# A one-core hybrid layer kernel: convolution taps loaded by a step of their own, the four short vectors loaded and turned with the biases

## The chip, the cores and the metric

The kernel runs on one core of a Trainium2 chip. The metric is device time in microseconds (us) of one execution. The engines are TensorE (PE; its weight loads are listed as PEld), VectorE (DVE), ScalarE (ACT), GpSimd (POOL) and SyncE (SP). A row with a q behind the engine's name (SPq, ACTq) is work of that engine's queue: here the issue of a DMA.

## The reference

One layer of a diffusion backbone: tokens x (1024 x 1024, float32) and 256 context tokens are RMS-normalised and modulated by vectors computed from `c` and `c_ctx`; the result is projected; half of the width goes through a convolution module, the other half through attention; both are gated and projected out.

```python
mod = jax.nn.silu(c) @ w_mod + b_mod                  # w_mod: 1024 x 3072
shift, scale, gate = jnp.split(mod, 3, axis=-1)
u = rms_norm(x, norm_w) * (1.0 + scale) + shift
p = u @ w_in
...
def conformer_conv(glu_in, conv_w, conv_b, ln_w, ln_b, w_pw, b_pw):
    a, g = jnp.split(glu_in, 2, axis=-1)
    u = a * jax.nn.sigmoid(g)
    y = conv(u, conv_w) + conv_b                      # depthwise, 31 taps, 512 channels
    y = jax.nn.silu(layer_norm(y, ln_w, ln_b))
    return y @ w_pw + b_pw
```

The change concerns `conv_w` (31 x 512, the taps) and the four vectors of 512 numbers, `conv_b`, `conv_ln_w`, `conv_ln_b` and `b_pw`. The kernel needs them per channel, one channel to a partition, so it loads them as rows and turns them by a matmul against the identity.

## The kernel before

The program has a start, a projection stage, attention, and an output stage. Every matrix product is made of three float32r products: an operand is split into a high part (name ending in h, made by ACT) and a low part (ending in l, the difference, made by DVE or POOL).

The start does three things at once. It computes the modulation in eight groups of columns (numbered by j, 0 to 7), it normalises and turns the eight tiles of tokens, and it computes the first GLU product (tiles a and g) from each group j as soon as its modulated tokens exist. It is a list of steps, `START`, whose letters mean:

- L j loads the columns of `w_mod` of group j (tiles wm; from group 3 on wm3s, wm4s, ...; four DMAs each, issued by SP); T j splits them; C j multiplies them with silu(c) (tile mrow, L264); D j copies the row (mrs, on DVE), turns it (mcol) and adds the biases (modc).
- X loads four token tiles, Q and R normalise one. P turns one group of one half of the tokens (xt), U modulates and splits it (u, uh, ul), M multiplies it (a, g).
- W loads the weights of the first GLU block, S splits them.
- V (`vectors`) loads the taps (cwrow) and the four vectors (vrow), turns both into the PSUM tile pcw, and copies them to cw and vcol.

Steps ahead of the bar in `START` are kept in the order written. From the bar on, a scheduler with a cost model of its own orders the instructions of each engine, so that a change of one step can move others; engines then run their instructions strictly in that order. Before the list, `setup` loads c, c_ctx, b_mod and norm_w (tiles crow and brow) and turns them.

Each DMA that SP or ACT issues is given one of eight completion semaphores in turn, by the build (named DMAHW0 to DMAHW7 in the orders below; the _49 behind them is the same for all). The issue waits until the DMA that had this semaphore before has landed. So at most eight such DMAs are under way, small or large, and a queue whose next DMA has to wait holds up all that stands behind it on that engine. These semaphores are called lanes below.

The first taps run on DVE when the first GLU block is done (`glu`, L453 and L456), and vcol is read there, in the layer norm (L511) and behind the pointwise product (L534). In the output stage, ln_stats turns y (yt, L480), ln_swish turns the normalised n (nt, L509) and makes s, sh and sl; `pointwise` (pw, L531) reads these; out_mm (o, L820) is the last product.

Of the kernel before, what the change touches and what calls it, by code (L numbers as in the profile page):

```python
# [9 lines left out]
F32 = mybir.dt.float32  # L10
# [8 lines left out]
P = 128  # L19
# [7 lines left out]
CW = 31  # L27
PAD = (CW - 1) // 2
EPS = 1e-6
Q0, K0, ZA0, A0, G0, ZC0 = 0, 512, 768, 1280, 1792, 2304  # L30
# [42 lines left out]
START = (  # L73
# [7 lines left out]
class Layer:  # L81
# [56 lines left out]
    def setup(self):  # L138

        nc, a, cst = self.nc, self.a, self.cst  # L140
        row = lambda ap, n: ap.rearrange("o (r f) -> (o r) f", f=P)[0:n]
        crow = self.w2([16, P], "crow")
        brow = self.w2([24, P], "brow")
        nc.sync.dma_start(out=crow[0:8], in_=row(a["c"], 8))
        nc.scalar.dma_start(out=crow[8:16], in_=a["c_ctx"].rearrange("(r f) -> r f", f=P))
        nc.scalar.dma_start(out=brow[0:16], in_=row(a["b_mod"], 16))
        nc.scalar.dma_start(out=brow[16:24], in_=row(a["norm_w"], 8))
        self.ident = ident = cst.tile([P, P], F32, name="ident")
        make_identity(nc, ident)
# [15 lines left out]
        pb = self.bank("t", "pb")  # L165
        nc.tensor.transpose(out=pb[:, 0:24], in_=brow, identity=ident[0:24, 0:24])
        self.bcol = bcol = cst.tile([P, 24], F32, name="bcol")
        nc.vector.tensor_copy(out=bcol[:, 0:8], in_=pb[:, 0:8])
        nc.vector.tensor_scalar(out=bcol[:, 8:16], in0=pb[:, 8:16], scalar1=1.0, scalar2=None, op0=ALU.add)
        nc.vector.tensor_copy(out=bcol[:, 16:24], in_=pb[:, 16:24])  # L170
        self.modc = cst.tile([P, NK, 4], F32, name="modc")

    def vectors(self):

        nc, a, cst = self.nc, self.a, self.cst
        row = lambda ap, n: ap.rearrange("o (r f) -> (o r) f", f=P)[0:n]
        vrow = self.w2([16, P], "vrow")
        cwrow = self.w2([CW, 512], "cwrow")
        for i, n in enumerate(("conv_b", "conv_ln_w", "conv_ln_b", "b_pw")):
            nc.sync.dma_start(out=vrow[4 * i:4 * i + 4], in_=row(a[n], 4))  # L180
        nc.sync.dma_start(out=cwrow, in_=a["conv_w"].rearrange("o w c -> (o w) c"))
        pw = self.bank("t", "pcw")
        for b in range(4):
            nc.tensor.transpose(out=pw[:, b * 32:b * 32 + CW], in_=cwrow[:, b * P:(b + 1) * P],
                                identity=self.ident[0:CW, 0:CW])
        nc.tensor.transpose(out=pw[:, 128:144], in_=vrow, identity=self.ident[0:16, 0:16])
        self.cw = cst.tile([P, 4, 32], F32, name="cw")
        nc.vector.tensor_copy(out=self.cw[:, :, 0:CW],
                              in_=pw[:, 0:128].rearrange("p (b w) -> p b w", w=32)[:, :, 0:CW])
        self.vcol = cst.tile([P, 16], F32, name="vcol")  # L190
        nc.vector.tensor_copy(out=self.vcol, in_=pw[:, 128:144])

# [752 lines left out]
    def start(self, w_in):  # L945
# [18 lines left out]
        def scale(i):  # L964
# [3 lines left out]
                 "Q": lambda i: r.update({i: self.norm_stats(self.xs[i])}), "R": scale,  # L968
                 "P": self.turn_x, "V": self.vectors, "U": self.make_u, "M": mm}
        first, rest = START.split("|")  # L970
# [99 lines left out]
```

## Time and profile before

| what | value |
|---|---|
| median of 3 runs | 688.29 us (686.16 to 690.2) |
| the profiled execution | 690.57 us |
| its span in the profile | 688.8 us (1.77 us lie around it) |
| mean granted TensorE clock | 0.989 |

The profiled execution is 2.28 us above the median. The span is what the views below divide up. An engine's share of busy time is an average over stages that have different limits; for a change in the start, the rows of the start decide. In a row of a timeline the bracket says how long the engine was idle before it and what ended the wait.

### The profile page before, as it was taken

The page shows a single profiled execution, that of the slowest core. Times are in us where ns is not written, and L with a number is a line of the kernel's source. Part 1 is how long each engine was busy: PE and PEld are TensorE (multiplying, and loading weights), DVE is VectorE, ACT ScalarE, POOL GpSimd, SP SyncE. Part 2 cuts the span into 40 slices and gives each one's busy share as a digit, 9 for nine tenths or more (in the row PEclk, how much of TensorE's full clock was granted, in tenths as well). Part 3 has the DMA queues.
Part 4 walks back from the last instruction along what each step waited for, and adds up shares of the span by engine and source line. Part 5 has one row for each costly group of instructions (what it writes and reads, how often), then busy time and mean ns, then how long its engine had stood idle before and what let it go on. Part 6 is the DMA issues. An engine that isn't in the chain of part 4 may idle for free.

```text
span 688.8 us, 11008 instructions
## 1 busy us (share of the span) xinstructions
PE 654.2 (95%) x4259; PEld 576.0 (84%) x4259; DVE 537.1 (78%) x844; ACT 352.2 (51%) x578; POOL 330.5 (48%) x289
## 2 busy tenths in 40 slices
PE   5979999999999999998999999999999989999997
PEld 1457899888888999997899998888888868888886
DVE  2678789839999999867999999999999953545422
ACT  3644424555343112235888888888888744332100
POOL 1233813967329132885657666655665754201200
PEclk9999999999999999999999999999999999999999
DMA  8973320311653232000010001011100021233711
GB/s 276 314 212 98 118 62 1 93 30 62 214 183 123 76 104 67 31 1 1 1 32 1 19 23 53 1 31 32 32 1 1 1 93 30 83 101 124 258 62 46
DMA packets 51251, 53.28 MB, mean 77 GB/s; under 512 B 4521, under 2 KB 41697, under 8 KB 51200
## 3 DMA queue, kind: packets, MB, share of 16 engines
q1 hardware_dynamic: 51136, 52.58, 24.3%
q8 instruction: 33, 0.54, 0.3%
q14 instruction: 18, 0.15, 0.1%
q10 hardware_dynamic: 64, 0.02, 0.0%
HBM read 44.20 MB, written 8.39 MB: 76 GB/s over the span
## 4 chain that ended last, share of the span: by engine, by line
PE 66%; DVE 24%; DMA 3%; issue 3%; ACT 2%; SPq 1%; POOL 0%; DVEq 0%; ACTq 0%
PE o L820 12%; PE pv L715 8%; PE s L636 7%; PE pt L682 7%; DVE y L456 6%; PE g L386 6%; PE a L386 6%; PE kv L412 4%; DVE yp L456 4%; PE pw L531 3%; PE zc L386 3%; PE q L412 3%; DVE p L700 3%; DVE nm L654 2%; DMA wm<-in_w_mod 2%
## 5 line engine op out<-in xcount | busy, mean ns | idle before, releaser
L706 POOL TENSOR_TENSOR p<-raw,p 128x512 fp32r<-128x512 f32 x96 | 127.0, 1337 | 81.7 <-DVE p L700 71.1
L636 PE MATMUL s<-kT,qT 128*128 128x512 f32 (+1 forms) x384 | 101.6, 375 | 3.8 <-ACT e L672 3.7
L715 PE MATMUL pv<-p,v 128*128 128x256 f32 x640 | 103.4, 293 | 0.7 <-DVE mm L747 0.7
L456 DVE SCALAR_TENSOR_TENSOR yp<-up,cw,yp 128x1024 f32<-128x1024 f32 x77 | 99.1, 1287 | 1.9
L682 PE MATMUL pt<-ident,e 128*128 128x128 f32 x640 | 94.4, 275 | 1.1 <-DVE p L706 0.9
L672 ACT ACTIVATE e<-s,nm 128x1280 f32<-128x1280 f32 x64 | 85.0, 1328 | 14.6 <-DVE nm L665 14.3
L715 PEld LDWEIGHTS pv<-p,v 128*128 128x128 f32 x640 | 86.2, 189 | 4.4 <-DVE mm L747 1.5
L654 DVE TENSOR_REDUCE nm<-s 128x1 f32<-128x1024 f32 x64 | 77.7, 1214 | 0.5
L682 PEld LDWEIGHTS pt<-ident,e 128*128 128x128 f32 x640 | 74.1, 142 | 2.7 <-PE pv L715 1.2
L636 PEld LDWEIGHTS s<-kT,qT 128*128 128x128 f32 x384 | 63.5, 191 | 10.6 <-ACT e L672 4.7
L691 ACT ACTIVATE raw<-pt 128x512 f32<-128x512 f32 x96 | 57.2, 598 | 10.2 <-PE pt L682 5.7
L700 DVE CAST p<-raw 128x512 fp32r<-128x512 f32 x96 | 47.3, 520 | 1.9 <-ACT raw L691 1.2
L698 ACT ACTIVATE p<-pt 128x512 fp32r<-128x512 f32 x64 | 38.5, 601 | 11.6 <-PE pt L682 10.2
L706 DVE TENSOR_TENSOR p<-pt,p 128x512 fp32r<-128x512 f32 x64 | 40.9, 676 | 1.4 <-ACT p L698 1.4
L456 DVE SCALAR_TENSOR_TENSOR y<-up,cw,y 128x1024 f32<-128x1024 f32 x25 | 40.9, 1635 | 0.8
L833 DVE TENSOR_TENSOR r<-o,gb 128x512 f32<-128x512 f32 (+1 forms) x17 | 10.8, 656 | 31.3 <-PE o L820 31.3
L659 DVE TENSOR_REDUCE nm<-s 128x1 f32<-128x256 f32 x64 | 26.9, 421 | 9.0 <-PE s L636 7.7
L441 POOL TENSOR_TENSOR yz<-yz,ct 128x512 f32<-128x512 f32 x24 | 33.6, 1433 | 0.0
L123 POOL TENSOR_TENSOR qr<-qr,mhalf 128x8 f32<-128x8 f32 (+1 forms) x13 | 21.2, 1631 | 8.7 <-DVE qr L122 8.4
L116 POOL TENSOR_TENSOR ul<-u,uh 128x512 fp32r<-128x512 f32 x8 | 11.2, 1405 | 27.4 <-DVE uh L114 26.0
L440 ACT ACTIVATE ct<-up,cw 128x512 f32<-128x512 f32 x24 | 15.7, 713 | 12.4 <-DVE up L424 9.9
L665 DVE TENSOR_TENSOR nm<-nm 128x1 f32<-128x1 f32 x64 | 20.3, 317 | 1.6
(580 smaller groups left out, 1758.1 us busy)
## 6 DMA issues: line engine op xcount, KB each, us to landing
x<-in_x SPq DMA_DIRECT2D x8, 512.0 KB, 7.0
wg<-in_w_mod SPq DMA_DIRECT2D x8, 512.0 KB, 4.1
xr<-in_x SPq DMA_DIRECT2D x8, 512.0 KB, 9.0
out<-r SPq DMA_DIRECT2D x15, 256.0 KB, 2.2
wm<-in_w_mod SPq DMA_DIRECT2D x12, 256.0 KB, 6.1
zc_d<-zc SPq DMA_DIRECT2D x4, 512.0 KB, 3.2
za_d<-za SPq DMA_DIRECT2D x4, 512.0 KB, 3.9
zar<-za_d SPq DMA_DIRECT2D x4, 512.0 KB, 3.9
```

The source lines that it names most:

```text
L386: nc.tensor.matmul(acc[h], lhsT=ww, rhs=uu[k][:, h * 512:(h + 1) * 512], start=first and i == 0, stop=last and i == 2)
L412: self.nc.tensor.matmul(acc[:, t * 256:(t + 1) * 256], lhsT=x, rhs=y, start=k == 0 and i == 0, stop=k == NK - 1 and i == 2)
L456: nc.vector.scalar_tensor_tensor(out=out, in0=up[:, w:w + S], scalar=cw[:, w:w + 1], in1=y if w else st["y2"], op0=ALU.mult, op1=ALU.add)
L636: mm = nc.tensor.matmul(self.s5[:, s0 + k0:s0 + k0 + n], lhsT=qt[:, h % 4, t * P:(t + 1) * P], rhs=kT[:, w, k0:k0 + n], start=w == 0, stop ...
L654: r = self.nc.vector.reduce_max(out=nm[:, 0:1], in_=self.s5[:, 1536 * t:1536 * t + 1024], axis=AX.X, negate=True)
L672: ex = nc.scalar.activation(e, self.s5[:, t * KEYS:(t + 1) * KEYS], AF.Exp, bias=st["nm", t][:, 2:3], accum_out=st["z"][:, t:t + 1])
L682: nc.tensor.transpose(out=tp[:, i * 256 + t * P:i * 256 + (t + 1) * P], in_=st["e", t][:, (2 * k + i) * P:(2 * k + i + 1) * P], identity=s ...
L691: self.nc.scalar.activation(raw, st["T", k], AF.Copy)
L700: nc.vector.tensor_copy(out=st["p", k][:, 0], in_=st["T", k])
L706: eng.tensor_sub(out=p[:, 1], in0=st["T", k], in1=p[:, 0].bitcast(F32))
L715: nc.tensor.matmul(st["pv"][:, 0:256], lhsT=self.v[:, kt, u[1] // 4].rearrange("p w d -> p (w d)"), rhs=st["p", k][:, j, i * 256:(i + 1) * ...
L820: self.nc.tensor.matmul(o, lhsT=p, rhs=q, start=half == k == i == 0, stop=half == 1 and k == 3 and i == 2)
```

## The change

The step V is parted. A new step Y (`tap_rows`) only issues the DMA of the taps; it stands behind L2, the load of the third group of modulation columns, in the part of `START` whose order is kept. V (`taps`) turns the taps and copies them. The four vectors are loaded by `setup`, from ACT's queue, into sixteen more rows of brow; they are turned by the matmul that turns the biases, which now has 40 rows where it had 24, and are copied to vcol there.

```diff
--- before.py
+++ after.py
@@ -71,7 +71,7 @@
 MODF = 3
 TLO = ['dp', 'pp', 'pp', 'dd', 'dd', 'dd', 'pd', 'dd']
 START = (
-    "L0 X0 L1 Q0 C0 W0 X1 Q1 L2 D0 Q2 R2 R0 L3 L4 Q3 R3 S0 | R1 C1 P00 P10 U00 W1 Q5 D1 M00 Q6 Q7 Q4 U10 R5 R4 R6 "
+    "L0 X0 L1 Q0 C0 W0 X1 Q1 L2 Y D0 Q2 R2 R0 L3 L4 Q3 R3 S0 | R1 C1 P00 P10 U00 W1 Q5 D1 M00 Q6 Q7 Q4 U10 R5 R4 R6 "
     "P20 R7 C2 M10 T3 P01 P11 V D2 U01 M01 P21 U11 C3 L5 M11 T4 D3 U20 C4 T5 U21 M21 M20 D4 L6 P30 U30 M30 C5 S1 "
     "P31 D5 T6 U31 L7 M31 P40 P50 U40 P41 M40 U41 C6 T7 D6 U50 M41 C7 P60 P51 D7 U51 U60 M50 P61 U61 M60 M51 P70 "
     "U70 P71 M61 U71 M70 M71"
@@ -140,11 +140,13 @@
         nc, a, cst = self.nc, self.a, self.cst
         row = lambda ap, n: ap.rearrange("o (r f) -> (o r) f", f=P)[0:n]
         crow = self.w2([16, P], "crow")
-        brow = self.w2([24, P], "brow")
+        brow = self.w2([40, P], "brow")
         nc.sync.dma_start(out=crow[0:8], in_=row(a["c"], 8))
         nc.scalar.dma_start(out=crow[8:16], in_=a["c_ctx"].rearrange("(r f) -> r f", f=P))
         nc.scalar.dma_start(out=brow[0:16], in_=row(a["b_mod"], 16))
         nc.scalar.dma_start(out=brow[16:24], in_=row(a["norm_w"], 8))
+        for i, n in enumerate(("conv_b", "conv_ln_w", "conv_ln_b", "b_pw")):
+            nc.scalar.dma_start(out=brow[24 + 4 * i:28 + 4 * i], in_=row(a[n], 4))
         self.ident = ident = cst.tile([P, P], F32, name="ident")
         make_identity(nc, ident)
         self.identr = cst.tile([P, P], F32R, name="identr")
@@ -163,32 +165,30 @@
         nc.vector.tensor_copy(out=cv[:, 0], in_=scv)
         nc.vector.tensor_sub(out=cv[:, 1], in0=scv, in1=cv[:, 0].bitcast(F32))
         pb = self.bank("t", "pb")
-        nc.tensor.transpose(out=pb[:, 0:24], in_=brow, identity=ident[0:24, 0:24])
+        nc.tensor.transpose(out=pb[:, 0:40], in_=brow, identity=ident[0:40, 0:40])
         self.bcol = bcol = cst.tile([P, 24], F32, name="bcol")
         nc.vector.tensor_copy(out=bcol[:, 0:8], in_=pb[:, 0:8])
         nc.vector.tensor_scalar(out=bcol[:, 8:16], in0=pb[:, 8:16], scalar1=1.0, scalar2=None, op0=ALU.add)
         nc.vector.tensor_copy(out=bcol[:, 16:24], in_=pb[:, 16:24])
+        self.vcol = cst.tile([P, 16], F32, name="vcol")
+        nc.vector.tensor_copy(out=self.vcol, in_=pb[:, 24:40])
         self.modc = cst.tile([P, NK, 4], F32, name="modc")
 
-    def vectors(self):
-
-        nc, a, cst = self.nc, self.a, self.cst
-        row = lambda ap, n: ap.rearrange("o (r f) -> (o r) f", f=P)[0:n]
-        vrow = self.w2([16, P], "vrow")
-        cwrow = self.w2([CW, 512], "cwrow")
-        for i, n in enumerate(("conv_b", "conv_ln_w", "conv_ln_b", "b_pw")):
-            nc.sync.dma_start(out=vrow[4 * i:4 * i + 4], in_=row(a[n], 4))
-        nc.sync.dma_start(out=cwrow, in_=a["conv_w"].rearrange("o w c -> (o w) c"))
+    def tap_rows(self):
+
+        self.cwrow = self.w2([CW, 512], "cwrow")
+        self.nc.sync.dma_start(out=self.cwrow, in_=self.a["conv_w"].rearrange("o w c -> (o w) c"))
+
+    def taps(self):
+
+        nc = self.nc
         pw = self.bank("t", "pcw")
         for b in range(4):
-            nc.tensor.transpose(out=pw[:, b * 32:b * 32 + CW], in_=cwrow[:, b * P:(b + 1) * P],
+            nc.tensor.transpose(out=pw[:, b * 32:b * 32 + CW], in_=self.cwrow[:, b * P:(b + 1) * P],
                                 identity=self.ident[0:CW, 0:CW])
-        nc.tensor.transpose(out=pw[:, 128:144], in_=vrow, identity=self.ident[0:16, 0:16])
-        self.cw = cst.tile([P, 4, 32], F32, name="cw")
+        self.cw = self.cst.tile([P, 4, 32], F32, name="cw")
         nc.vector.tensor_copy(out=self.cw[:, :, 0:CW],
                               in_=pw[:, 0:128].rearrange("p (b w) -> p b w", w=32)[:, :, 0:CW])
-        self.vcol = cst.tile([P, 16], F32, name="vcol")
-        nc.vector.tensor_copy(out=self.vcol, in_=pw[:, 128:144])
 
     def tables(self):
 
@@ -966,7 +966,7 @@
         steps = {"L": self.mod_load, "X": tokens, "W": lambda h: st.update({h: self.w_stage(w_in, wcol, "wglu0", h)}),
                  "S": split, "T": self.mod_split, "C": self.mod_mm, "D": self.mod_cols,
                  "Q": lambda i: r.update({i: self.norm_stats(self.xs[i])}), "R": scale,
-                 "P": self.turn_x, "V": self.vectors, "U": self.make_u, "M": mm}
+                 "P": self.turn_x, "Y": self.tap_rows, "V": self.taps, "U": self.make_u, "M": mm}
         first, rest = START.split("|")
         with self.tc.manual_schedule():
             for step in first.split():
```

What this does to the orders is shown at three places.

**The queues of DMAs.** First SP before, at the loads of wm4s (group 4), the vectors, the taps and the first loads of wm5s (group 5); a bracket names the semaphores that a row waits for, and four rows are left out in the middle:

```order
L215 DMA wm4s_202<-in_w_mod 128x4x128 [waits DMAHW6_49]
L215 DMA wm4s_202<-in_w_mod 128x4x128 [waits DMAHW7_49]
L215 DMA wm4s_205<-in_w_mod 128x4x128 [waits DMAHW0_49]
L215 DMA wm4s_205<-in_w_mod 128x4x128 [waits DMAHW1_49]
...
L180 DMA vrow<-in_conv_b 4x128 [waits DMAHW6_49,Activation_49]
L180 DMA vrow<-in_conv_ln_w 4x128 [waits DMAHW7_49]
L180 DMA vrow<-in_conv_ln_b 4x128 [waits DMAHW0_49]
L180 DMA vrow<-in_b_pw 4x128 [waits DMAHW1_49]
L181 DMA cwrow<-in_conv_w 31x512 [waits DMAHW2_49,DVE_49,PE_49]
L215 DMA wm5s_394<-in_w_mod 128x4x128 [waits DMAHW3_49]
L215 DMA wm5s_394<-in_w_mod 128x4x128 [waits DMAHW4_49]
```

And SP now, from the end of L2 on:

```order
L180 DMA cwrow<-in_conv_w 31x512 [waits DMAHW6_49]
L215 DMA wm3s_204<-in_w_mod 128x4x128 [waits DMAHW7_49]
...
L215 DMA wm4s_210<-in_w_mod 128x4x128 [waits DMAHW3_49]
L215 DMA wm4s_210<-in_w_mod 128x4x128 [waits DMAHW4_49]
L215 DMA wm4s_213<-in_w_mod 128x4x128 [waits DMAHW5_49]
L215 DMA wm4s_213<-in_w_mod 128x4x128 [waits DMAHW6_49]
...
L215 DMA wm5s_392<-in_w_mod 128x4x128 [waits DMAHW3_49]
L215 DMA wm5s_392<-in_w_mod 128x4x128 [waits DMAHW4_49]
L215 DMA wm5s_395<-in_w_mod 128x4x128 [waits DMAHW5_49]
L215 DMA wm5s_395<-in_w_mod 128x4x128 [waits DMAHW6_49]
```

The taps' row has moved up past the loads of groups 3 and 4; the four rows of vrow are gone from SP, and the four loads of wm5s stand on the lanes that the four loads of wm4s had. ACT's first rows before:

```order
L145 DMA crow<-in_c_ctx 8x128
L146 DMA brow<-in_b_mod 16x128
L147 DMA brow<-in_norm_w 8x128
L159 ACT_TABLE_LOAD
L159 ACTIVATE sc<-pc 128x16 [waits PE_49]
```

And now:

```order
L145 DMA crow<-in_c_ctx 8x128
L146 DMA brow<-in_b_mod 16x128
L147 DMA brow<-in_norm_w 8x128
L149 DMA brow<-in_conv_b 4x128
L149 DMA brow<-in_conv_ln_w 4x128 [waits DMAHW1_49]
L149 DMA brow<-in_conv_ln_b 4x128 [waits DMAHW3_49]
L149 DMA brow<-in_b_pw 4x128 [waits DMAHW5_49]
L161 ACT_TABLE_LOAD
L161 ACTIVATE sc<-pc 128x16 [waits PE_49]
```

Four DMAs have come in ahead of ACT's table load, and three of them wait for a lane: DMAHW1, 3 and 5 are those of c_ctx, b_mod and norm_w, in this order.

**PE at the turning of the taps**, before (a and g are the first GLU block, mcol turns the modulation of group 3, and the last two rows begin that of group 4):

```order
L386 MATMUL g_120<-ul_287,wglu00h 128x512
L386 MATMUL g_120<-uh_286,wglu00l 128x512
L386 MATMUL a_118<-ul_287,wglu00h 128x512
L386 MATMUL a_118<-uh_286,wglu00l 128x512
L184 MATMUL pcw<-ident,cwrow 128x31 x4
L186 MATMUL pcw<-ident,vrow 128x16
L276 MATMUL mcol_416<-ident,mrs_414 128x4 x2
L264 MATMUL mrow_429<-wm40h,chl 4x256
L264 MATMUL mrow_429<-wm40l,chl 4x256
```

And now, from the first GLU matmuls of group 0 on the second half of the tokens:

```order
L386 MATMUL g_126<-uh_248,wglu00h 128x512
L386 MATMUL a_124<-uh_248,wglu00h 128x512
L264 MATMUL mrow_375<-wm31h,chl 4x256
L187 MATMUL pcw<-ident,cwrow 128x31 x4
L386 MATMUL g_126<-ul_249,wglu00h 128x512
L386 MATMUL g_126<-uh_248,wglu00l 128x512
L386 MATMUL a_124<-ul_249,wglu00h 128x512
L386 MATMUL a_124<-uh_248,wglu00l 128x512
L264 MATMUL mrow_375<-wm31l,chl 4x256
```

The four matmuls of the taps stand some 18 rows further up, ahead of ul's matmuls and of the rest of group 3's modulation; the row of vrow is gone. Behind this place, up to the end of the start, the scheduler has also put transposes xt and GLU matmuls in another order on PE, and splits and copies on DVE and ACT; their number is the same.

**PE in the output stage**, at the last turned tiles (nt) of the layer norm, before:

```order
L509 MATMUL nt_6999<-ident,n_6968 128x128 x2
L509 MATMUL nt_7009<-ident,n_6968 128x128 x2
L820 MATMUL o_7165<-wo03h,mcl_6885 128x512
L820 MATMUL o_7165<-wo03h,mch_6884 128x512
L820 MATMUL o_7165<-wo03l,mch_6884 128x512
L820 MATMUL o_7165<-wo03h,mcl_6885 128x512
L531 MATMUL pw_7021<-sh_6997,wp0h 128x256
```

And now:

```order
L509 MATMUL nt_6997<-ident,n_6966 128x128 x2
L820 MATMUL o_7163<-wo0h,mah_5221 128x512
L820 MATMUL o_7163<-wo0l,mah_5221 128x512
L820 MATMUL o_7163<-wo0h,mal_5222 128x512
L509 MATMUL nt_7007<-ident,n_6966 128x128 x2
L820 MATMUL o_7163<-wo0h,mah_5221 128x512
L820 MATMUL o_7163<-wo0l,mah_5221 128x512
L820 MATMUL o_7163<-wo0h,mal_5222 128x512
L820 MATMUL o_7163<-wo1h,mah_5221 128x512
L820 MATMUL o_7163<-wo1l,mah_5221 128x512
L820 MATMUL o_7163<-wo1h,mal_5222 128x512
L820 MATMUL o_7163<-wo1h,mah_5221 128x512
```

Before, four output matmuls stand between the last nt and the pointwise product that needs what ACT and DVE make of it; now there are 33 (the first five are seen here). Between the end of the start and the output stage no engine's order has changed.

## Rows read from the trace of the kernel before

**Rows 1.** Busy us (instructions) of each engine by stage, granted clock, DMA share, GB/s

```profile
76.00:205.00 129.00, 129.00 (x716) 112.30 (x715) 109.65 (x118) 54.60 (x89) 67.43 (x50) 1.00 0.27 88
205.00:290.00 85.00, 84.51 (x649) 81.28 (x648) 81.38 (x64) 19.99 (x29) 45.61 (x26) 1.00 0.25 78
...
560.00:689.00 129.00, 120.79 (x644) 102.74 (x642) 53.85 (x100) 28.69 (x49) 23.69 (x18) 0.98 0.29 98
```

**Rows 2.** The chain that ended last, first 82 us: start us, us, what

```profile
17.26 8.69 DMA wm<-in_w_mod
...
26.09 3.69 PE mrow L264 x16
...
35.58 5.54 DMA cwrow<-in_conv_w
...
41.82 1.73 PE mrow L264 x9
...
54.35 0.44 PE xt L343 x4
...
62.45 1.71 PE mrow L264 x15
```

**Rows 3.** PE's timeline there: start us, us, what [idle before <-releaser]

```profile
37.33 0.39 PE L386 MATMUL a<-uh,wglu00l 128*128 128x512 f32 x1
41.25 0.41 PE L184 MATMUL pcw<-ident,cwrow 31*128 31x31 f32 x4 [3.53 <-DMA cwrow<-in_conv_w]
```

**Rows 4.** DVE's timeline there

```profile
37.58 0.41 DVE L273 COPY mrs<-mrow 4x256 f32<-4x256 f32 x1
...
43.70 1.23 DVE L116 TENSOR_TENSOR wm50l<-wm5s,wm50h 128x1024 fp32r<-128x1024 f32 x1 [0.58 <-ACT wm50h L112]
45.83 0.41 DVE L273 COPY mrs<-mrow 4x256 f32<-4x256 f32 x1 [0.91 <-PE mrow L264]
```

**Rows 5.** ACT's timeline there

```profile
42.60 1.06 ACT L112 ACTIVATE wm50h<-wm5s 128x1024 fp32r<-128x1024 f32 x1 [6.09 <-DMA wm5s<-in_w_mod]
```

**Rows 6.** Stretches of 5 us, columns as in rows 1

```profile
35.00:40.00 5.00, 2.45 (x13) 1.34 (x11) 4.03 (x6) 1.51 (x2) 1.29 (x1) 1.00 0.72 202
40.00:45.00 5.00, 3.75 (x24) 2.86 (x25) 2.59 (x7) 1.56 (x2) 0.00 (x0) 0.71 0.85 243
```

**Rows 7.** SP's timeline of DMA issues

```profile
21.45 5.31 SPq L215 DMA_DIRECT2D wm3s<-in_w_mod  x4
...
32.79 0.61 SPq L180 DMA_DIRECT2D vrow<-in_conv_b  x1
33.45 0.29 SPq L180 DMA_DIRECT2D vrow<-in_conv_ln_w  x1
...
35.58 0.23 SPq L181 DMA_DIRECT2D cwrow<-in_conv_w  x1
35.85 2.88 SPq L215 DMA_DIRECT2D wm5s<-in_w_mod  x4
```

**Rows 8.** The first 16 us, all engines

```profile
1.72 0.36 ACTq L147 DMA_DIRECT2D brow<-in_norm_w  x1
2.11 1.28 ACT L159 ACT_TABLE_LOAD   x1 [2.11 <-issue]
...
2.64 0.26 PE L157 MATMUL pc<-ident,crow 16*128 16x16 f32 x1 [2.64 <-DMA crow<-in_c]
...
5.09 1.86 PE L264 MATMUL mrow<-wm,sc 128*2 128x256 f32 x4 [2.19 <-DMA wm<-in_w_mod]
...
15.58 3.18 PE L264 MATMUL mrow<-wm,sc 128*2 128x256 f32 x8 [2.61 <-DMA wm<-in_w_mod]
```

**Rows 9.** The tile brow, issue to landing

```profile
DMA to landing us min/median/max: 2.2/2.2/2.2
```

**Rows 10.** DMA from 10 to 30 us

```profile
DMA packets 8429, 6.70 MB, mean 335 GB/s; under 512 B 321, under 2 KB 7717, under 8 KB 8429
```

**Rows 11.** PE's waits from 575 to 640 us: us, times, longest

```profile
PE pw L531 <- DVE sl L116: 0.6, 2, 0.3
```

## The prediction

> **What bounds the kernel now.** I read the busy time by stage first. PE is full from 76 to 205 us (129.00 of 129 us) and from 205 to 290 us (84.51 of 85); the output stage leaves 8.2 us of 129 [rows 1]. Whatever moves the end of the start, at about 76 us, is therefore handed on by a PE that has no slack, in an order that does not change there. So the start decides.
>
> The chain of waits shows three parts of the start [rows 2]. Up to 25.95 us (17.26 and 8.69) it is the DMA stream, ending with the third group of modulation columns. Then PE works from 26.09 on. At 35.58 the chain leaves PE: for 5.54 us it is the DMA of the taps. The PE timeline shows the hole: the last GLU matmul starts at 37.33 and takes 0.39, then nothing runs until the taps are turned at 41.25, 3.53 us that the bracket gives to cwrow [rows 3]. PE's clock falls behind it: granted 0.71 of full speed on the mean from 40 to 45 us, which must be a mix of the levels 1.2 and 2.4 GHz [rows 6].
>
> **The change, part by part.**
>
> *The wait for the taps (gain).* The taps are needed only when the first GLU block is done, at the end of the start, but PE runs in order, so group 4's modulation stands behind them. Without that wait, the next row is mcol, which needs DVE's copy mrs, started at 37.58 and 0.41 long [rows 4]. PE could go on at about 38.0 instead of 41.25: 3.53 - 0.3 = 3.2 us. The four turning matmuls keep their 0.41 us, elsewhere on PE; the matmul for vrow, a fraction of that, joins one that is there already.
>
> *The clock (gain).* Group 4's sixteen matmuls and four transposes lie between 41.82 [rows 2] and 45.83, where DVE's mrs waits for the last of them [rows 4]: 4.0 us. At full clock, fifteen such matmuls take 1.71 us and four transposes 0.44 [rows 2], so this work takes 16 x 0.114 + 0.44 = 2.3 us. The fall came behind an idle stretch of 3.5 us; with 0.3 us idle I expect none. Gain 1.7 us. Group 4 is then done 4.9 us sooner, at about 40.9.
>
> *What is late next (loss).* DVE copies group 4's row (mrs) only behind the split wm50l, in both orders. wm50l waits for ACT's wm50h, and that waited 6.09 us for the load of wm5s and started at 42.60 [rows 5]. From there to the end of wm50l are 2.33 us (43.70 + 1.23 - 42.60) [rows 4]. The loads of wm5s were issued from 35.85 on, behind the vectors, issued from 32.79 on [rows 7]. The vectors' lanes were those of the four loads of wm4s; the loads of wm5s now have exactly these. So they can go where the vectors went, 3.06 us sooner. If they take as long to land as before, wm50h starts at 39.5, wm50l ends at 41.9 and mrs runs then instead of at 45.83: 3.9 us sooner. Of the 4.9 us, 1.0 is lost again. Bounds: nothing lost (4.9), if the loads land faster without five small ones among them; or only 1.7 us sooner, if the DMA engines are the limit (second rival). I take 3.9, because they are not full: their share is 0.72 from 35 to 40 us, against 0.85 in the next stretch [rows 6].
>
> *The taps' new place (small loss).* Their DMA goes behind L2, and PE meets them 18 rows sooner: at about 34 us, and not ahead of 30.7 even if each of these took the 0.39 us of a GLU matmul (37.72 - 18 x 0.39) [rows 3]. The load of group 2 that was issued at 17.26 took 8.69 us to land [rows 2]; with as much, taps issued where wm3s began, at 21.45 [rows 7], land at 30.1: in time. Ahead of wm3s they cost their issue, 0.23 us [rows 7], which shifts wm3s and wm4s by 0 to 0.25; I take 0.1.
>
> *Four DMAs on ACT's queue (hidden).* They stand ahead of the table load and of sc, which the first modulation matmul needs. The wait for c_ctx is over by 2.64, when PE's pc had crow. norm_w, issued at 1.72 [rows 8], lands 2.2 us later [rows 9]; the last new issue waits for it, so it ends at about 4.3 (3.9 + 0.36). The table load takes 1.28, sc a fraction of that, so the first mrow starts near 5.9 instead of 5.09 [rows 8]. Group 0's sixteen matmuls move by 0.8 us, and behind them PE idled 2.61 us for the load of group 1, until 15.58 [rows 8]: that covers it. If norm_w landed as late as the load in [rows 2], 8.7 us, the cover would be gone and some 3.5 us lost; but nothing new lies ahead of it. The matmul that turns brow now stands behind group 0, which ended at 12.97 (15.58 - 2.61) and now ends near 13.8, so even 8.7 us of landing for the last vector (4.3 + 8.7 = 13.0) leaves it hidden. One more small copy on DVE hides there as well.
>
> *The lanes in the first 12 us (small loss).* The four small DMAs take four of eight lanes in turn. The first token load now waits for a lane of group 0's first load, which landed at the latest at 5.09 [rows 8], and group 1's third load for that of the first tokens. From 10 us on the engines are full anyway, 335 GB/s [rows 10], so only a gap ahead of that counts: 0 to 1 us, taken as 0.3.
>
> *The output stage (either way).* The last layer norm now has 33 matmuls of cover where it had four. PE's waits for sl in this stretch were 0.6 us [rows 11], and other places get less cover. I take a gain of 0.3, between -1.0 and +1.1 (estimates from the idle in [rows 1, 11]).
>
> **Sum.** 3.9 - 0.1 - 0.3 + 0.3 = 3.8 us. Against the profiled execution, 690.57, that gives 686.8; that one is 2.28 above the median, so for the median of 688.29 I predict 684.5 us, -0.55%.
>
> **The rivals.**
>
> *All of it is won.* wm5s lands early enough, and the output stage gains: 4.9 + 1.1 = 6.0 us, 682.3. For it: five small DMAs are gone from a stream that ran below its rate [rows 6]. Against it: nothing shows that landing times shrink. 0.14.
>
> *The DMA engines are the limit.* wm5s then comes sooner only by the issue time taken off SP: 0.61 + 3 x 0.29 + 0.23 = 1.7 us [rows 7] (three vectors at the price of the one shown). With the small terms that is a gain of 1.6: 686.7. Against it: the share of 0.72. For it: 0.85 just behind [rows 6]. 0.20. The Trainium skill speaks for this one: "DMA: Bandwidth & Descriptors", section "Issuing engines are not separate DMA queues", says that DMAs of all issuing engines run on the same 16 DMA engines, so that another queue saves only the time of issuing. By that rule alone the sum would be this rival's; the trace agrees only where the engines are full.
>
> *It does not do what it says.* The taps are late at their new place too, or the hole passes to another load of that stretch: 688.3. It takes a landing of over 9.2 us (30.7 - 21.45) [rows 3, 7], against 8.69 [rows 2]. 0.06.
>
> *Slower: the start starves.* If the lanes held by small DMAs let the stream fall from 335 GB/s [rows 10] to the 202 seen where five small ones were under way [rows 6], the 5.3 MB between 10 and 25.95 us take 26.4 us instead of 15.95, and the third group lands 10.5 us later: 688.29 + 10.5 - 3.8 = 695.0. It decides below 270 GB/s, where 5.3 MB take 3.8 us more. Against it: the small DMAs come once, and each landed in 2.2 us [rows 9]. 0.08.
>
> **How the numbers follow.** The forecast has 0.52, with a range of its own from 683.2 to 685.7. The range for 8 in 10 goes from 681.8 to 687.6: it holds the forecast and the first two rivals, and leaves out the last two (0.14) and the outer ends. Half a per cent, 3.4 us, is about what a measurement of this kernel can tell from no change; the line lies at 684.85, inside the forecast. Two thirds of it (0.35), nearly all of the first rival and a little of the second are faster: 0.50; slower 0.08; within, 0.42.
>
> **What would show it.** Right: no idle of PE over 1 us between 36 and 46 us; the clock granted in full there; wm50h near 39.5; the end of the start, with the first tap on DVE behind it, some 4 us sooner. The loss is where I put it if DVE's mrs of group 4 follows wm50l at once while PE has been done with its matmuls. The third group landing near 26 shows the lanes harmless; at 30 or later, the last rival. Wrong would be a gain that is gone by 76 us because DVE and POOL set the pace behind group 4, or an output stage that is longer by a microsecond or more.

## The result

| | median | range of the times | executions |
|---|---|---|---|
| before | 689.08 us | 685.86 to 692.06 | 20 |
| changed | 684.56 us | 683.55 to 688.53 | 20 |

The ratio is 0.9946 (95% interval 0.993 to 0.9961), a gain of 0.54%; one disturbed execution of the changed kernel, of 919.71 us, is left out of the range and of the ratio, while the median of 20 has it in (684.52 without it). The medians are 4.5 us apart, the means, without that execution, 3.8. The predicted 684.5 us is met, but by luck: most of the gain lies in the output stage, where 0.3 us had been predicted.

**The start of the changed kernel.** SP's issues of DMAs, then PE at the taps:

```profile
21.45 1.27 SPq L180 DMA_DIRECT2D cwrow<-in_conv_w  x1
22.76 4.27 SPq L215 DMA_DIRECT2D wm3s<-in_w_mod  x4
27.08 4.73 SPq L215 DMA_DIRECT2D wm4s<-in_w_mod  x4
...
35.06 2.48 SPq L215 DMA_DIRECT2D wm5s<-in_w_mod  x4
```

```profile
35.01 0.43 PE L187 MATMUL pcw<-ident,cwrow 31*128 31x31 f32 x4
39.53 0.28 PE L276 MATMUL mcol<-ident,mrs 4*128 4x4 f32 x2 [0.32 <-DVE mrs L273]
```

The bracket at pcw is gone ([rows 3] had 3.53), and mcol waits 0.32. But the taps' issue took 1.27 us and not 0.23, and wm5s is issued 0.8 us sooner than in [rows 7], not 3. (The rows left out are the two norm weights and wglu0s, whose issue took 1.97 us here and 1.03 before.) ACT, DVE and POOL:

```profile
31.16 1.06 ACT L112 ACTIVATE wm30h<-wm3s 128x1024 fp32r<-128x1024 f32 x1 [2.60 <-DMA wm3s<-in_w_mod]
...
40.50 1.07 ACT L112 ACTIVATE wm50h<-wm5s 128x1024 fp32r<-128x1024 f32 x1 [1.36 <-DMA wm5s<-in_w_mod]
```

```profile
41.88 1.26 DVE L284 TENSOR_SCALAR modc<-mt,bcol 128x2 f32<-128x2 f32 x1
43.06 0.27 DVE L286 TENSOR_SCALAR modc<-mt,bcol 128x2 f32<-128x2 f32 x1
43.25 1.21 DVE L116 TENSOR_TENSOR wm50l<-wm5s,wm50h 128x1024 fp32r<-128x1024 f32 x1
44.39 0.41 DVE L273 COPY mrs<-mrow 4x256 f32<-4x256 f32 x1
...
47.10 2.17 DVE L284 TENSOR_SCALAR modc<-mt,bcol 128x2 f32<-128x2 f32 x1
...
72.73 1.35 DVE L453 TENSOR_SCALAR yp<-up,cw,vcol 128x1024 f32<-128x1024 f32 x1
```

```profile
41.36 1.76 POOL L116 TENSOR_TENSOR ul<-u,uh 128x512 fp32r<-128x512 f32 x1 [3.40 <-DVE mt L280]
46.35 2.89 POOL L116 TENSOR_TENSOR wm60l<-wm6s,wm60h 128x1024 fp32r<-128x1024 f32 x1 [3.23 <-ACT wm60h L112]
```

DVE is now what PE follows: group 4's mrs stands directly behind wm50l, at 44.39 and not at 45.83 [rows 4], and the first tap is at 72.73; before, it was at 75.10 in the same view. The stretches of 5 us that [rows 6] shows, and the stages, with the window moved by what the start gained:

```profile
35.00:40.00 5.00, 4.68 (x31) 3.44 (x31) 5.00 (x7) 3.09 (x4) 1.47 (x2) 1.00 0.96 272
40.00:45.00 5.00, 5.00 (x35) 4.13 (x33) 5.00 (x10) 3.42 (x4) 1.76 (x1) 1.00 1.14 292
...
73.00:202.00 129.00, 129.00 (x716) 112.27 (x715) 109.83 (x117) 55.31 (x89) 67.38 (x50) 1.00 0.27 88
202.00:287.00 85.00, 84.58 (x647) 81.19 (x646) 81.68 (x64) 19.05 (x27) 45.67 (x25) 1.00 0.24 76
553.00:682.00 129.00, 122.06 (x670) 104.85 (x668) 56.54 (x104) 31.48 (x53) 25.40 (x21) 0.99 0.29 102
```

PE is full and at full clock from 40 to 45 us, and the DMA share has risen to 0.96 and 1.14, from 0.72 and 0.85 in [rows 6]. The first two stages are what they were in [rows 1]. The first 16 us, too, hide what was put there, as [rows 8] let expect:

```profile
4.52 1.28 ACT L161 ACT_TABLE_LOAD   x1 [4.52 <-DMA brow<-in_conv_ln_b]
...
6.05 6.07 PE L264 MATMUL mrow<-wm,sc 128*2 128x256 f32 x16 [3.33 <-ACT sc L161]
...
15.57 1.01 PE L264 MATMUL mrow<-wm,sc 128*2 128x256 f32 x2 [0.78 <-DMA wm<-in_w_mod]
```

**Where the 7.1 us between the two profiled spans (688.8 and 681.7) lie.** The table has every kernel of this study: the first tap (DVE, yp), the granted clock just behind the place of the old wait, the time from the start of the first weight load of yt to the start of the last r that is made from o (the output stage), and the clock in it.

| kernel | first tap | clock 40 to 44 us | first yt to last r | clock 565 to 570, 570 to 575 | span |
|---|---|---|---|---|---|
| before | 75.10 | 0.77 | 129.9 | 0.78, 0.88 | 688.8 |
| before again (e7) | 72.63 | 1.00 | 128.3 | 1.00, 1.00 | 684.1 |
| changed | 72.73 | 1.00 | 125.6 | 1.00, 1.00 | 681.7 |
| changed again (e11) | 73.06 | 1.00 | 127.2 | 0.66, 1.00 | 684.5 |
| e1 | 75.24 | 0.50 | 125.6 | 1.00, 1.00 | 684.0 |
| e6 (e1 again) | 75.10 | 0.50 | 125.6 | 1.00, 1.00 | 684.0 |
| e2 | 76.42 | 0.57 | 129.9 | 0.97, 0.69 | 690.0 |
| e3 | 73.09 | 1.00 | 125.6 | 1.00, 1.00 | 682.2 |
| e4 | 80.23 | 0.55 | 127.0 | 1.00, 0.78 | 690.9 |
| e5 | 72.43 | 1.00 | 127.2 | 0.66, 1.00 | 683.8 |
| e8 | 75.70 | 0.82 | 125.6 | 1.00, 1.00 | 685.5 |
| e9 | 75.70 | 1.00 | 127.1 | 0.87, 0.78 | 687.0 |
| e10 | 75.89 | 1.00 | 127.1 | 0.77, 0.89 | 686.1 |
| e12 | 72.76 | 1.00 | 125.6 | 1.00, 1.00 | 682.8 |

Of 7.1 us, 2.4 lie ahead of the first tap, 4.3 in the output stage, and about 0.4 in attention. The clock also falls at a third place, in attention at 319 to 331 us, in every row of the table but changed, e3 and e10; the last section has it.

### The profile page after: what moved, and what is told of

Its sections match the earlier page's. It is cut to its first block, busy times and chain, and to the rows that moved or that the text cites. A ratio compares the mean times of both kernels' runs of the same rounds, so it can differ in the third digit from the quotient of the medians.

```text
span 681.7 us, 11003 instructions
## 1 busy us (share of the span) xinstructions
PE 650.2 (95%) x4258; PEld 572.3 (84%) x4258; DVE 537.4 (79%) x844; ACT 352.9 (52%) x578; POOL 332.5 (49%) x289
## 4 chain that ended last, share of the span: by engine, by line
PE 67%; DVE 23%; issue 3%; DMA 3%; ACT 2%; SPq 1%; POOL 0%; DVEq 0%; ACTq 0%
PE o L820 12%; PE pv L715 8%; PE s L636 8%; PE pt L682 7%; DVE y L456 6%; PE g L386 6%; PE a L386 6%; PE kv L412 4%; DVE yp L456 4%; PE pw L531 3%; PE zc L386 3%; PE q L412 3%; DVE p L700 3%; DVE nm L654 2%; DMA wm<-in_w_mod 2%
## 5 line engine op out<-in xcount | busy, mean ns | idle before, releaser
L706 POOL TENSOR_TENSOR p<-raw,p 128x512 fp32r<-128x512 f32 x96 | 127.0, 1337 | 81.2 <-DVE p L700 70.8
```

The lines of the kernel that those rows point to most:

```text
L706: eng.tensor_sub(out=p[:, 1], in0=st["T", k], in1=p[:, 0].bitcast(F32))
```

## The experiments

**e1 and e6: the output stage's order alone.** One ScalarE copy that nothing reads makes the scheduler put the output stage in the changed order, row for row on PE, DVE, ACT and POOL; all ahead of it stays.

```diff
+                self.dm = self.cst.tile([P, P], F32, name="dm")
+                add(TAIL + 15, lambda: self.nc.scalar.activation(self.dm[:, 0:128], self.ones[:, 0:128], AF.Copy))
                 self.attention(hooks)
```

> The kernel before with one small ScalarE copy (128x128, into a tile that nothing reads) added in the output stage. The loads, turns and taps at the start stand exactly as before; the order of the instructions in the output stage becomes that of the changed kernel. Theory (the order of the output stage is worth 2.7 us by itself): first tap near 75 us as before, the stretch from the first yt to the last r about 2.7 us shorter than in the kernel before, about 686.3 us where the kernel before has 689, ratio 0.996. Rival (the 4.3 us that the output stage lost between the two profiles were a lower clock in one of them, and its order is worth nothing): ratio 1.000, within 0.1%.

Measured: 684.8 us, ratio 0.995 (0.9926 to 0.9973): the theory held, and more. The first tap is at 75.24, and yet the time is that of the changed kernel: 683.49 us at the least, where the changed kernel has 683.55. So the start's 2.4 us had to be looked at again, with more executions in the profile.

> e1 once more, for another execution in the profile. e1's times lie in groups near 683.6, 686 and 688.5 us. Theory B: if the profiled execution is one of 683.6 us, TensorE's wait for the taps is still there with about 3 us, its clock is granted in full from 40 to 48 us, and the first tap stands at 72.9 us. Theory A: in such an execution the first tap still stands at 75 us, and the 2.4 us to the next group lie elsewhere. If it is one of 686 us, it repeats e1's rows: clock 0.5 from 40 to 44 us, first tap at 75.2.

> The kernel before once more, for another execution in the profile. Theory B: an execution near 686.2 us has its first tap near 72.9 us, one near 688.6 has lost the clock in one of two places, behind the wait for the taps or in the output stage from 565 to 575 us, and one near 691 in both, as in the profile shown. Theory A: the first tap stands at 75 us whatever the time. Either way the output stage from the first yt to the last r takes 128.4 us with the full clock from 565 to 575 us, 2.8 more than in e1.

e6 fell on an execution of 686 us and repeats e1's rows, ratio 0.9968 (0.9943 to 0.9994). e7 is the kernel before in an execution of 685.86 us. Its PE, DVE and ACT:

```profile
25.64 5.85 PE L264 MATMUL mrow<-wm,sc 128*2 128x256 f32 x16 [0.78 <-DMA wm<-in_w_mod]
...
39.42 0.40 PE L386 MATMUL a<-uh,wglu00l 128*128 128x512 f32 x1
39.75 0.43 PE L184 MATMUL pcw<-ident,cwrow 31*128 31x31 f32 x4
```

```profile
42.33 1.23 DVE L116 TENSOR_TENSOR wm50l<-wm5s,wm50h 128x1024 fp32r<-128x1024 f32 x1 [0.69 <-ACT wm50h L112]
43.48 0.41 DVE L273 COPY mrs<-mrow 4x256 f32<-4x256 f32 x1
...
72.63 1.35 DVE L453 TENSOR_SCALAR yp<-up,cw,vcol 128x1024 f32<-128x1024 f32 x1
```

```profile
41.24 1.06 ACT L112 ACTIVATE wm50h<-wm5s 128x1024 fp32r<-128x1024 f32 x1 [3.47 <-DMA wm5s<-in_w_mod]
```

In e7 the clock fell earlier than in the first profile of before, so that the third group's sixteen matmuls took 5.85 us and not 3.69 [rows 2]; a stretch of e7 and then one of e1, the granted clock third from the right, 0.50 being the lower of its two levels (1.2 GHz):

```profile
24.00:28.00 4.00, 3.22 (x9) 0.90 (x8) 2.98 (x7) 2.64 (x5) 2.31 (x3) 0.50 1.22 290
```

```profile
40.00:44.00 4.00, 3.38 (x20) 2.69 (x21) 2.25 (x7) 1.06 (x1) 0.00 (x0) 0.50 0.87 249
```

In e7 PE comes to the taps 2 us later, does not wait for them, and keeps the full clock from 36 to 48 us. The first tap comes at 72.63: the kernel before reaches it as soon as the changed one, in such an execution. In e1 PE waits, and its mrs comes late:

```profile
40.62 0.60 PE L184 MATMUL pcw<-ident,cwrow 31*128 31x31 f32 x4 [2.98 <-DMA cwrow<-in_conv_w]
```

```profile
45.89 0.41 DVE L273 COPY mrs<-mrow 4x256 f32<-4x256 f32 x1 [1.54 <-PE mrow L264]
```

But the wait and the fall are not all that differs. In e7 the loads, too, are sooner: the taps are issued at 34.71 us and not at 35.58, and wm50h starts at 41.24 and not at 42.60 [rows 5], 1.36 of the 2.47 us between the two first taps; why, stays open. DVE's bracket at mrs says how long, behind the split wm50l, it still waited for PE's late work: 0.91 us in the first profile [rows 4], 1.54 in e1 and 1.65 in e6. That is what the wait and the fall cost at this place; most of the rest came with the loads. No profile caught e1 in one of its fastest executions, so that its first tap comes early there, too, is inferred from the times.

The output stage of e7 has the old order at full clock: 128.3 us, against 125.6 in the changed order. The old order with the fall takes 129.9, so the fall costs 1.6, and so it does in the changed order (e11, 127.2). The order is worth 2.7 us. Where, PE's rows of e7 show, at the last nt:

```profile
617.68 0.39 PE L820 MATMUL o<-wo03h,mcl 128*128 128x512 f32 x1
618.55 0.39 PE L531 MATMUL pw<-sh,wp0h 128*128 128x256 f32 x1 [0.48 <-ACT sh L112]
618.78 0.28 PE L531 MATMUL pw<-sh,wp1h 128*128 128x256 f32 x1
619.34 0.39 PE L531 MATMUL pw<-sl,wp0h 128*128 128x256 f32 x1 [0.28 <-DVE sl L116]
```

and those of the changed kernel at the same place:

```profile
616.57 0.39 PE L820 MATMUL o<-wo03h,mcl 128*128 128x512 f32 x1
616.80 0.28 PE L531 MATMUL pw<-sh,wp0h 128*128 128x256 f32 x1
616.91 0.28 PE L531 MATMUL pw<-sh,wp1h 128*128 128x256 f32 x1
617.03 0.28 PE L531 MATMUL pw<-sl,wp0h 128*128 128x256 f32 x1
```

Read the starts and not the brackets: an o takes 0.23 from start to start, a pw 0.12, so the two gaps of e7 are 0.87 - 0.23 = 0.64 and 0.56 - 0.12 = 0.44 us. Two more such places, at 576 us (nt, behind DVE's ma) and 602 us (sl), have 0.46 and 0.45. That is 2.0 of the 2.7 us; the brackets of the same places give 1.35, and the waits for sl alone, on which the prediction rested, 0.6 [rows 11]. Part of the rest are the matmuls right behind a gap, which take longer (the pw of 618.55 takes 0.23 to the next start and not 0.12).

**e2 and e3: each half of the change.** e2 leaves the taps' load in V, behind W1's loads; e3 leaves the four vectors there, and moves the taps only.

```diff
 # e2
-... L2 Y D0 ...
+... L2 D0 ...
     def taps(self):
+        self.tap_rows()
 # e3, against the kernel before
-... L2 D0 ...
+... L2 Y D0 ...
     def vectors(self):
-        nc.sync.dma_start(out=cwrow, in_=a["conv_w"].rearrange("o w c -> (o w) c"))
```

> The changed kernel with the taps loaded and turned at their old place, behind the gate's first weights; only the four vectors are loaded and turned with the biases. Theory (the wait for the taps is what held TensorE, and it stays): TensorE waits about 3 us at the taps, first tap at 74 to 75 us, the output stage's order and length as before, ratio 0.999 to 1.000. Rival (the four small transfers ahead of the taps made them late, so that they land in time without them): TensorE's wait at the taps under 1.5 us, first tap at 73 us, ratio 0.997.

> The kernel before with the taps moved behind the third group of modulation columns, as in the changed kernel, and the four vectors still loaded by four transfers and turned at their old place. Theory (the wait goes over to the vectors' turn): TensorE waits 2 us or more at the vectors' turn, first tap at 74 us or later, output stage 2.7 us shorter by its order, ratio 0.996. Rival (the four small transfers land quickly and the taps alone were the wait): no wait over 0.7 us at the turn of the vectors, first tap at 72.7 us as in the changed kernel, ratio 0.9945.

e2: 690.3 us, ratio 1.0031 (1.0012 to 1.0049). PE waits as the theory said, but the first tap, at 76.42, is a microsecond later than in before, and the ratio is above the 1.000 that the theory allowed.

```profile
40.56 0.59 PE L188 MATMUL pcw<-ident,cwrow 31*128 31x31 f32 x4 [2.76 <-DMA cwrow<-in_conv_w]
```

e3: 684.95 us, ratio 0.9938 (0.9917 to 0.9959). The rival held: the vectors' turn does not wait.

```profile
40.15 0.23 PE L190 MATMUL pcw<-ident,vrow 16*128 16x16 f32 x1
```

The taps' move, with the order that it brings in the output stage, is the whole gain. Moving the vectors gives nothing beside it that can be measured, and by itself (e2) it makes the kernel slower by 0.3%; the scheduler orders the start otherwise there, too, so why stays open.

**e5: the taps' matmuls without their wait.** e1's kernel, whose taps' matmuls read a tile that is there:

```diff
-            nc.tensor.transpose(out=pw[:, b * 32:b * 32 + CW], in_=cwrow[:, b * P:(b + 1) * P],
+            nc.tensor.transpose(out=pw[:, b * 32:b * 32 + CW], in_=self.ident[0:CW, 0:P],
```

> The kernel of e1 (loads as in the kernel before, output stage in the changed order), in which the matmuls that turn the taps read the identity's rows and not the loaded taps; the taps are still loaded at their old place, into a tile that nothing reads, so the convolution here uses wrong taps. It takes only TensorE's wait for the taps away. Theory A (the wait costs in every execution, and the changed kernel gave 1.3 us of it back by loading the taps ahead of group 3): no idle of TensorE over 1 us between 36 and 46 us, first tap at 71.3 to 72 us, least time about 680.5 us, 1 us or more under the 683.5 of e1 and of the changed kernel. Theory B (without the wait VectorE sets the pace; the wait only makes a fall of the clock likelier, and an execution without that fall loses nothing by it): first tap at 72.5 to 73 us, least time 683.5 us as in e1, median 683.5 to 684.2.

684.88 us, ratio 0.9954 (0.9931 to 0.9978), at the least 683.27: the times are theory B's, but for the median, since this kernel, too, has a fall of the clock in the output stage (0.66 from 565 to 570 us). It is not the wait alone that was taken away, though: with nothing to wait for, the scheduler ordered about a hundred rows of PE in the start otherwise than in e1, and in this execution the loads run some 0.9 us ahead of e1's (wm3s issued at 20.52, and 21.40 in e1). So e5 agrees with theory B and does not settle it. Its ACT and DVE show what is late next:

```profile
41.47 1.06 ACT L112 ACTIVATE wm50h<-wm5s 128x1024 fp32r<-128x1024 f32 x1 [3.00 <-DMA wm5s<-in_w_mod]
```

```profile
42.56 1.23 DVE L116 TENSOR_TENSOR wm50l<-wm5s,wm50h 128x1024 fp32r<-128x1024 f32 x1 [1.29 <-ACT wm50h L112]
43.71 0.41 DVE L273 COPY mrs<-mrow 4x256 f32<-4x256 f32 x1
```

**e4 and e8: what the taps' transfer costs ahead of group 3.** e4 moves the step Y behind L4; e8 is e1's kernel with the taps loaded a second time at the changed place.

```diff
 # e4
-... L2 Y D0 Q2 R2 R0 L3 L4 Q3 ...
+... L2 D0 Q2 R2 R0 L3 L4 Y Q3 ...
 # e8, against e1
-... L2 D0 ...
+... L2 Y D0 ...
+        self.cwrow0 = self.w2([CW, 512], "cwrow0")
+        self.nc.sync.dma_start(out=self.cwrow0, in_=self.a["conv_w"].rearrange("o w c -> (o w) c"))
```

> The changed kernel with the taps' step one place later: their transfer is issued behind the loads of the fourth group of columns and not ahead of them. Theory (ahead of those loads the taps' transfer costs 1.3 to 1.5 us, by its issue of 1.27 us and by what it delays behind it): the eviction wm30h is back at 29.7 us from 31.2, first tap at 71.4 us, 1.3 sooner than in the changed kernel, ratio 0.9925. Rival (the transfer costs the same wherever it stands, or the taps land late and TensorE waits for them again): first tap at 72.7 us or later, ratio 0.9945 or above.

> The kernel of e1 with one more load of the taps behind the third group's loads, where the changed kernel has its own, into a tile that nothing reads; the old load and the wait for it stay. Theory (ahead of the loads of group 3 the transfer costs 1.3 to 1.5 us): its issue takes about 1.3 us, the eviction wm30h starts near 31.2 us and not at 29.7, and the first tap comes 0.5 to 1.5 us later than in e1 at the same clock. Rival (in the changed kernel another thing made wm3s late, the vectors or the lanes): wm30h stays at 29.7 us.

e4: 689.71 us, ratio 1.002 (1.0001 to 1.004). The taps' issue takes 0.36 us there and wm30h starts at 29.63, as the theory said, but the scheduler orders the start otherwise: PE waits 3.24 us for DVE's uh at 40.62, and the first tap comes at 80.23. So e4 says nothing on the whole price. e8: 688.98 us, ratio 1.0015 (0.9993 to 1.0038), 3.0 us above e6, the same kernel as e1 measured beside it. wm30h comes at

```profile
30.67 1.06 ACT L112 ACTIVATE wm30h<-wm3s 128x1024 fp32r<-128x1024 f32 x1 [3.33 <-DMA wm3s<-in_w_mod]
```

and at 29.56 in e1: one transfer of 31 rows (62 KB) put the loads behind it back by 1.1 us. Executions are shifted against each other, so it is better counted from the first load of the third group: 13.7 us in e8, and 12.7 to 13.0 in the nine profiles that have no transfer at this place, 0.7 to 1.0 more. The kernels with the changed place (changed, e3, e11, e12) have 14.5 to 15.4, so e8 shows half of the price or less. The spans of the two profiles differ by 1.5 us; why the medians differ by more stays open, but more than the transfer differs: the scheduler has ordered some eighty rows of PE in the start otherwise than in e1.

**e9, e10 and e11: a later place.** e9 loads the taps behind L5 and turns them behind D6, e10 behind L7 and C7; e11 is the changed kernel again.

```diff
 # e9
-... L2 Y D0 ... P11 V D2 ... C3 L5 M11 ... T7 D6 U50 ...
+... L2 D0 ... P11 D2 ... C3 L5 Y M11 ... T7 D6 V U50 ...
```

> The changed kernel with the taps needed and loaded late: they are loaded behind the loads of group 5 and turned at the end of the start (behind D6), so that nothing of groups 3 to 7 waits for them and no load of groups 3 to 5 stands behind them; the output stage keeps the changed order. Theory B (with TensorE's wait gone VectorE and the loads of group 5 set the pace, and the clock decides the rest): first tap at 72 to 73 us, least time 683.3 to 683.7 us as in e1, e5 and the changed kernel, median within 1 us of the changed kernel's. Rival (the taps' transfer ahead of group 3 still costs the changed kernel 1 us or more in every execution): eviction wm30h at 29.6 us, first tap under 71.7 us, least time under 682.7 us, median 683.5 us or less.

> As e9, with the load of the taps behind the loads of group 7, the last of the modulation, so that no load of the modulation stands behind it; turned behind C7. Theory B: as e9, least time 683.3 to 683.7 us, first tap at 72 to 73 us. Rival 1 (every transfer taken out of the stream of loads gives its price back): least time 0.3 us or more under e9's. Rival 2 (so late, the taps land behind the first GLU block): VectorE waits for them at its copy cw, first tap at 74 us or later, median 686 us or more.

> The changed kernel once more, beside e9 and e10 on the same chip and for another execution in the profile. Theory B: times in the groups seen before, near 683.6, 686 and 688.5 us, median 684 to 686 us; if the profiled execution is near 683.6, the first tap stands at 72.7 us, and if it is near 686 or 688.5, the clock has fallen at a place from 36 us on where in the first profile it had not, and the stretch around it is longer by 1.5 to 2.5 us. Rival (the groups have another cause than the clock): an execution near 686 us shows its 2.4 us in a stretch with the full clock.

e9: 687.41 us, ratio 0.9986 (0.9972 to 1.0); e10: 687.34, 0.9983 (0.9967 to 0.9999). Both theories missed: the first tap comes at 75.7 and 75.9 with the full clock. The scheduler has ordered the start otherwise again (in more than a hundred rows on PE), and in e9 DVE waits 2.77 us for PE's mcol at 64.37, where e11 waits 0.85. The order that the scheduler happens to find weighs as much as the edit. e11: 686.1 us, ratio 0.996 (0.9936 to 0.9984); its profiled execution has the fall where theory B looks for it, in the output stage, and one in attention besides:

```profile
565.00:570.00 5.00, 4.22 (x21) 4.02 (x22) 2.38 (x6) 4.07 (x7) 0.32 (x1) 0.66 0.00 0
```

**e12: less on POOL.** In the changed kernel's rows above (modc is an addition, a TENSOR_SCALAR), the modc of 47.10 ends at 49.27 and POOL's wm60l at 49.24; the modc of 41.88 ends at 43.14 and POOL's ul at 43.12.

```diff
-TLO = ['dp', 'pp', 'pp', 'dd', 'dd', 'dd', 'pd', 'dd']
+TLO = ['dp', 'pp', 'pp', 'dd', 'dd', 'dd', 'dd', 'dd']
-        self.split(self.uh[j][:, sl], self.ul[j][:, sl], u, hi_on="dve", lo_on=("dve", "pool")[h])
+        self.split(self.uh[j][:, sl], self.ul[j][:, sl], u, hi_on="dve", lo_on=("dve", "pool" if j != 3 else "dve")[h])
```

> The changed kernel with two splits of the start moved from POOL to VectorE: wm60l (the first low part of group 6) and the low part ul of group 3's second half of the tokens. The order of the other instructions stays but for a dozen rows on TensorE, and the output stage keeps the changed order. In the changed kernel, VectorE's small modc of 128x2 took 2.17 us and ended when POOL's wm60l ended (49.27 and 49.24 us), and another took 1.24 us and ended with POOL's ul (53.96 and 53.94); alone it takes 0.22. Theory (VectorE sets the pace of the start from 36 to 56 us, and these waits for POOL are part of it): both modc take 0.2 to 0.3 us; VectorE does 1.2 + 0.7 us more and waits 1.95 + 1.0 less, so the first tap comes about 1.1 us sooner, at 71.6, and the least time is 682.5 us. Rival (the loads or TensorE set the pace): modc is short, but the first tap stays at 72.7 us or comes later, and the least time at 683.5 us or above.

684.02 us, ratio 0.9944 (0.992 to 0.9967), at the least 683.19: the lowest median here, but not apart from the changed kernel's. The modc that stood beside wm60l is short (the one ahead of wm50l, whose POOL neighbour the edit left alone, still takes 1.25):

```profile
47.95 0.23 DVE L284 TENSOR_SCALAR modc<-mt,bcol 128x2 f32<-128x2 f32 x1
```

The first tap is at 72.76, where the theory had 71.6; but in this execution group 4's mcol comes at 40.40, 0.87 late. From there to the first tap are 32.36 us, against 33.20 in both profiles of the changed kernel. So this stretch is 0.8 us shorter, where 1.1 were expected, in an execution that was late ahead of it (wm3s issued at 23.78, and at 22.76 in the changed kernel). That the first tap would come 0.8 sooner in another execution is not shown.

## Why the prediction was right, and where not

*The wait goes* (3.2): right, as a row. *The clock stays* (1.7): right in the profiles (1.00 from 40 to 45 us). But the prediction took one execution for the kernel: e7 shows that before, too, some executions have neither the wait nor the fall at the taps.

*What is late next* (group 4's mrs 3.9 us sooner): the mechanism is right, wm50l sets mrs; the size is wrong. wm5s was issued 0.8 us sooner, not 3.06: the place behind wglu0s, where the vectors had stood at 32.79, comes at 35.06, since the taps' issue had put all behind it back by about 1.3 us and wglu0s took 0.9 longer to issue. wm50h started at 40.50, not 39.5, and then wm50l stood behind a modc held up by POOL. mrs came 1.4 us sooner. In e5, which has the loads in the order of before, mrs comes at 43.71, 2.1 sooner, and the first tap at 72.43, with wm50h 1.1 sooner (41.47).

*The taps' new place* (0.1): mis-sized; wm30h starts 1.5 us later than the 29.65 of before, and e8 shows 0.7 to 1.1 of it by the transfer alone. *ACT's queue* (0) and *the lanes* (0.3): hidden, C1 at 15.57 and not 15.58 [rows 8], the third group's matmuls at 26.14 and not 26.09 [rows 2].

*The output stage* (0.3): this is the step that failed. It measured 2.7 us. The sum of waits for one tile was taken for the stage's idle time, while four places lost it, on sh and ma too; and matmul ends are modelled, so that each of the four brackets is too short by 0.16 us against the starts (0.48 for 0.64, 0.28 for 0.44). The bound of +1.1 did not hold it either. With it fails the sentence that "the start decides": e1 leaves the start as it was and has the changed kernel's time.

So the total was met by luck, because one term was too large and another too small. Over all executions (means): before 688.5 us (117), e1 and e6 685.6 (20), changed 685.4 (27). The order alone gives 2.9 us (2.0 to 3.7, by resampling the executions), and what the start gives beyond it is 0.1 (-0.9 to 1.1). Between the two profiles shown it gave 2.4 us at the first tap; in how many executions it gives anything, these runs don't settle.

Of the rivals, "the DMA engines are the limit" had the start best: its 1.7 us for mrs stands against 1.4, and the DMA share of 0.96 and 1.14 says that the DMA engines have no room left there. Its reason is not borne out in full: it had wm5s issued 1.7 us sooner, and it was 0.8. The Trainium skill ("DMA: Bandwidth & Descriptors", section "Issuing engines are not separate DMA queues") says that DMAs issued by any engine share the same 16 DMA engines, so that another queue saves the time of issuing alone. The runs agree: with the vectors on ACT's queue (changed, mean 685.4 us) or on SP's (e3, 684.8 in six executions) the times cannot be told apart. The starving start did not come.

## What to carry to other kernels

Where a scheduler writes the order, compare the order of the whole program after an edit, and price each place that moved by starts of neighbouring matmuls: the far place may carry the gain. A wait that is removed is worth only the time to what is late next, here a load and a split. And before a clock's fall is priced, take a second profile of the kernel before: it may not fall there each time.

## What the runs showed of the hardware

The same program's clock fell at different places: in the first profile of before behind 3.53 us of idle at the taps, in e7 earlier and not there; in e11 at 565 us and in the first profile of the same kernel not. In attention PE idles 2.73 us, waiting for ACT's e, in all 14 profiles (at 321.91 in before, at 319.72 in the changed kernel); at this place the clock fell to 0.50 in eleven of them and stayed at 1.00 in changed, e3 and e10.

A fall in the output stage costs 1.6 us. One in attention costs from nothing to 1.1: from the first tap to the first yt it is 479.2 to 480.6 us with it and 479.2 to 479.6 without, and e12 has the first tap and the output stage of the changed kernel and a span 1.1 longer. What the fall at the taps costs by itself no run shows; with the wait it held up mrs by 0.77 (e8) to 1.65 us (e6).

An addition of 128x2 on DVE (modc), 0.22 us alone, ends with POOL's running instruction, within 0.03 us, after 1.26 or 2.17 us. The Trainium skill, "SBUF — State Buffer", section "Who interferes with whom", says that a DVE instruction in a mode that uses both of its ports, which tensor_scalar can enter, contends with GpSimd: whichever issues first gets the shared ports for its whole instruction, and the other blocks. The rows agree: POOL started first both times (41.36 and 46.35, against 41.88 and 47.10), and in e12, with POOL's wm60l gone, modc takes 0.23. That modc runs in such a mode no run shows.

The issue of one and the same load of the taps took 0.23 us on SP at its old place, and 0.63 (e8), 1.27 (changed), 1.78 (e11), 1.93 (e3) and 2.28 us (e12) behind the third group's loads.
